# Modulation rows beside layer 0's gate and up: from column-group matmuls to VectorE, ScalarE and GpSimd

## The chip, the cores and the metric

One core of a Trainium2 chip runs the whole program in one launch. The metric is the device time of an execution in microseconds (us), lower is better; the figure of a kernel is the median of its runs. One further execution is recorded by the profiler, and all rows below come from it. The engines are TensorE (PE, with its weight loads as PEld), VectorE (DVE), ScalarE (ACT), GpSimd (POOL) and SyncE (SP), which issues the transfers spoken of here.

## What is computed

Two layers of a trunk, each with a mixer and a feed-forward part, on 1,024 latent and 128 context positions of width 1,024. What matters here is the modulation: for each layer 6 x 1,024 columns for two conditions (context and latent).

```python
silu_ctx = jax.nn.silu(c_ctx.astype(F32))
silu_c = jax.nn.silu(c.astype(F32))
for l in range(DEPTH):
    mod_ctx = (silu_ctx @ wa + ba)[None, None, :]
    mod_lat = (silu_c @ wa + ba)[:, None, :]          # wa: 1024 x 6144
    xp = layer(xp, mod_ctx, ...)
    xs = layer(xs, mod_lat, ...)

def layer(x, mod, p, ...):
    sh1, sc1, g1, sh2, sc2, g2 = jnp.split(mod, 6, axis=-1)
    h = rmsnorm(x, norm[0]) * (1.0 + sc1) + sh1
    m = mixer(h, ...)
    x = x + g1 * rmsnorm(m, norm[1])
    h = rmsnorm(x, norm[2]) * (1.0 + sc2) + sh2
    f = (silu(h @ w_gate) * (h @ w_up)) @ w_down      # hidden 2816
    return x + g2 * rmsnorm(f, norm[3])
```

The kernel multiplies the norm's weights into the modulation rows that scale (four of the six: `norm[0]` to `norm[3]` go with sc1, g1, sc2 and g2), so that such a row is (modulation + bias + 1 or 0) times a row of norm weights.

## The kernel before

The program is written with pools of buffers and a scheduler that puts each engine's instructions into a fixed order when the program is built; on the chip every engine works through its own order and waits on semaphores. The order of SP is that of the transfers. A layer goes through in-projection and mixer (phases 1 and 2), the output projection (phase 3), gate and up (`gate_up`), and the down projection (`ffn`). Layer 1's modulation rows are computed during layer 0's `gate_up`, where they aren't needed yet.

**Gate and up.** The hidden width is cut into units of 128 gate columns; `units` lists 24 of them, the first four over one half of the positions, 20 over both. A unit is a product of 2x2 blocks made with seven block products. For each, `prepare` makes the weight operand: sums of weight blocks on GpSimd (`ft`, and in place in the loaded weights; L158 is the helper for all additions of two tiles), then a split into a high part on ScalarE (L121) and a low part on VectorE (L126), both into a slot of `fw`. There are six such slots, and `prepare` runs five block products ahead of `product` (`AHEAD`). `product` runs, for each half of the positions (256 and 320 columns), 12 matmuls into one of six psum banks (`gu`; L130 to L132 are the three terms of the split), and an eviction that adds the bank to a running sum on VectorE (L158), the first of the seven a copy on ScalarE (L1449). A full unit so has 14 banks to empty, seven of 256 columns and seven of 320. After the seventh product come the tanh on ScalarE (L1456), two VectorE operations (L161) and the stores of `h` (L1461, L1463). The weights come with L1409, 512 KB each, into `fr` or spare tiles (`X`, `x`).

**Modulation beside it.** `gate_up` makes a generator `ada` and calls `next(ada)` once after each block product except a unit's first, from the fifth unit on: 120 calls. `ada_steps` goes through 24 chunks of 256 columns. A chunk's weights, 1,024 x 256, come in four loads of 256 KB into `adw` (three slots; L291). The eight row blocks are taken in two groups of four matmuls (L302): matmul j of a group uses 32 columns of the array (`tile_position`), its stationary operand is a slice of the constants that holds the silu of both conditions for its row block, and it writes 32 partitions of the bank `psada`. Then ScalarE copies the bank (L308), and `ada_total` sums: four more matmuls on the four column groups with a selection matrix as the stationary operand (L269) bring the sums of both conditions and both column halves onto one tile of 128 x 128; VectorE adds the bias row (L271), and for sc1, g1, sc2 and g2 (16 of the 24 chunks) multiplies with the norm row (L275). The bias row comes in two loads into `adr` (L264), which then holds the result; the norm row comes in two loads into a part of the `th` tile (L274); two stores bring the result to memory (`mods`, L278). `csilu` is the tile of the silu values, `konst` the constants in another layout.

In phase 1 of layer 0 the same generator computes layer 0's other rows.

Of the kernel before, what the change touches and what calls it, by code (L numbers as in the profile page):

```python
# [10 lines left out]
F32 = mybir.dt.float32  # L11
F32R = mybir.dt.float32r
I32 = mybir.dt.int32
AF = mybir.ActivationFunctionType
ALU = mybir.AluOpType
# [4 lines left out]
P = 128  # L20
L = 2
D = 1024
# [77 lines left out]
class Kern:  # L100
# [138 lines left out]
    def load_cond(self):  # L239
# [12 lines left out]
        nc.vector.tensor_reduce(out=self.sel, in_=self.ident.rearrange("p (j i) -> p i j", j=4)[:, 0:2], axis=AX.X, op=ALU.add)  # L252
        self.mods = {(l, s): self.dram([2, D], f"mod{l}_{s}") for l in range(L) for s in range(6)}

    def ada_total(self, l, c, r, ng, psp, tag, parts, by):


        nc, A = self.nc, self.A
        m = r.shape[-1]
        s, c0 = c // D, c % D  # L260
        k = {1: 0, 2: 1, 4: 2, 5: 3}.get(s)
        half = [slice(c0 + m * h, c0 + m * h + m) for h in range(2)]
        for h in range(2):
            nc.sync.dma_start(r[64 * h:64 * h + 64], A["bada"][l, s:s + 1, half[h]].broadcast_to([64, m]))  # L264
        ps = psp.tile([P, m], F32, name="psada", tag=tag)
        for h in range(2):
            for i in range(2):
                q = 64 * h + 32 * i
                nc.tensor.matmul(ps[q:q + 32], by[i], parts[i][:, m * h:m * h + m], start=True, stop=True,  # L269
                                 tile_position=(0, q))  # L270
        nc.vector.tensor_tensor(out=r, in0=ps, in1=r, op=ALU.add)  # L271
        if k is not None:
            for h in range(2):
                nc.sync.dma_start(ng[64 * h:64 * h + 64], A["normg"][l, k:k + 1, half[h]].broadcast_to([64, m]))  # L274
            nc.vector.scalar_tensor_tensor(out=r, in0=r, scalar=1.0 if s in (1, 4) else 0.0, in1=ng,  # L275
                                           op0=ALU.add, op1=ALU.mult)
        for h in range(2):
            nc.sync.dma_start(self.mods[l, s][:, half[h]], r[64 * h:64 * h + 64:32])  # L278

    def ada_steps(self, l, c0, n, pool, psp, tag, stage, bufs=2, rest=0):  # L280


        nc, A = self.nc, self.A
        quarters = [(c, q) for c in range(c0, 6 * D, n) for q in range(4)]
        ws = []

        def load():
            if len(ws) < len(quarters):
                c, q = quarters[len(ws)]
                w = pool.tile([P, 2, n], F32, name="adw", bufs=bufs)  # L290
                nc.sync.dma_start(w, A["wada"][l, 2 * q:2 * q + 2, :, c:c + n].rearrange("k p c -> p k c"))  # L291
                ws.append(w)

        for _ in range(bufs):
            load()
        for i in range(0, len(quarters), 2):
            c, q = quarters[i]
            if q == 0:
                ps = psp.tile([P, n], F32, name="psada", tag=tag)
            for j in range(4):  # L300
                kt = 2 * q + j
                nc.tensor.matmul(ps[32 * j:32 * j + 32], self.konst[:, kt:kt + 249:8], ws[i + j // 2][:, j % 2],  # L302
                                 start=q == 0, stop=q > 0, tile_position=(0, 32 * j))
            load()
            load()
            if q:
                cp = stage()[:, :n]
                nc.scalar.activation(cp, ps, AF.Copy)  # L308
            yield
            for _ in range(0 if q else rest):  # L310
                yield
            if q:
                r = pool.tile([P, n // 2], F32, name="adr")
                self.ada_total(l, c, r, cp[:, :n // 2], psp, tag, [cp] * 2,
                               [self.sel[:, k:k + 1].broadcast_to([P, 32]) for k in range(2)])
                yield
# [359 lines left out]
    def phase1(self, l):  # L676
        nc, tc, A = self.nc, self.tc, self.A
        with ExitStack() as c:
# [5 lines left out]
            adp = c.enter_context(tc.tile_pool(name="ada", bufs=1, reuse_waits="tile")) if l == 0 else None  # L684
            psp = Banks(c, tc, "ps1", {"tr": 2, "acc": 2, "psf": 3, "ad": 1} if l == 0 else {"tr": 2, "acc": 3, "psf": 3})
            if l == 0:
# [7 lines left out]
                ng = [h1p.tile([2, 512], F32, name="ng0", tag=tg) for tg in ("gc", "ginv")]  # L694
# [12 lines left out]
                for t0, n in ((0, 2), (2, 2), (4, 5)):  # L707
                    ss = h1p.tile([P, n], F32, name=f"ss0{t0}")
                    r = h1p.tile([P, n], F32, name=f"rs0{t0}")
# [7 lines left out]
                with tc.high_priority(offset=0):  # L717
                    for q in (0, 2, 1, 3):
                        ps = psp.tile([2, 512], F32, name="psada", tag="acc")
                        for j in range(4):  # L720
                            w = chunk(4 * q + j)
# [3 lines left out]
                        r = bias[q // 2][:, hs]  # L725
# [16 lines left out]
            for o in range(2):  # L742
                self.filter_spectrum(l, o, h1p, h2p, psp, "psf")
            widths = [288] + [256] * 4
            ada = self.ada_steps(0, 2 * D, 256, adp, psp, "ad",
                                  lambda: sp.tile([P, 512], F32, name="adc", tag="stg", bufs=3)) if l == 0 else iter(())

            def natural(i, kr=None):
# [630 lines left out]
    def gate_up(self, l, wr, wt, x8):  # L1379
        nc, tc, A = self.nc, self.tc, self.A  # L1380
# [3 lines left out]
        with ExitStack() as c:  # L1384
            banks = Banks(c, tc, "gu", {"ad": 2, "gu": 6})
            pool = lambda nm, bufs=1, **k: c.enter_context(tc.tile_pool(name=nm, bufs=bufs, reuse_waits="tile", **k))
# [3 lines left out]
            adp = None if last else pool("ada2")  # L1390
            x1.update({nm: pool(f"x1{nm}") for nm in ("a12", "s2", "s3", "s1", "a11")})
            if not last:
                ada = self.ada_steps(1, 0, 256, adp, banks, "ad", lambda: x8.tile([P, 2, 320], F32, name="th")[:, 0], 3, 1)
            for i, nm in enumerate(self.XOPS):
                if nm != "a12":
                    self.X[1][nm] = [x1[nm].tile([P, 4, 320], F32R, name=f"x1{nm}{h}") for h in range(2)]
            state, late = {}, []

            def load(u):

                f = units[u][0]
                if u == 1:
                    raw = [x1["a12"].tile([P, 8, P], F32, name=f"fr{i}", tag=f"x1a12{i}") for i in range(2)]
                elif u % 3 == 2 or u == 0:
                    raw = [wr.tile([P, 8, P], F32, name=f"fr{i}") for i in range(2)]
                else:
                    raw = self.spare[2 * (u % 3):][:2]
                for i in range(2):
                    nc.sync.dma_start(raw[i], A["wf"][l, f, :, 8 * i:8 * i + 8])  # L1409
                return raw  # L1410
# [54 lines left out]
            todo = [(u, i) for u in range(len(units)) for i in range(7)]  # L1465
            AHEAD = 5
            for k in range(len(todo) + AHEAD):
                if k < len(todo):
                    u, i = todo[k]
# [4 lines left out]
                if k >= AHEAD:  # L1474
                    u, i = todo[k - AHEAD]
# [252 lines left out]
```

## Time and profile before

| what | us |
|---|---|
| runs | 3404.67, 3415.93, 3424.79 |
| median | 3415.93 |
| the profiled execution | 3418.3 |
| its span in the trace | 3416.5 |
| TensorE busy in it | 3174.7 |
| VectorE, ScalarE, GpSimd busy | 2118.5, 1253.9, 439.0 |

The span is the time from the first to the last recorded instruction. A stretch of TensorE that is full at a granted clock of 1.00 can't get shorter unless it gets fewer columns to work on; the busy time of the other engines is a share of a long program with unlike stages, so the rows below are taken from the stage that changes: layer 0's gate and up runs from about 960 to 1,522 us of the profiled execution, and its modulation matmuls from 971.9 to 1,423 us.

### The profile page before, as it was taken

The numbers are of one execution on the slowest core, as the hardware profiler recorded it, in microseconds if no ns is written. First come the engines' busy times: TensorE is split into PE (matmuls) and PEld (weight loads), VectorE is DVE, ScalarE is ACT, GpSimd is POOL, SyncE is SP. The second block draws the span as 40 slices with busy tenths as digits, with TensorE's granted clock in tenths as the row PEclk, the third lists the DMA queues.
The fourth block names the chain that finished last, engine by engine and source line by source line (L and its number), as shares of the span: only waits on it lengthen the run. The fifth ranks groups of instructions, "written<-read, shape, count | busy, mean of one in ns | idle before, by whom it ended". The sixth has DMA issues, their size and how long they took to land.

```text
span 3416.5 us, 52623 instructions
## 1 busy us (share of the span) xinstructions
PE 3174.7 (93%) x19870; PEld 2795.5 (82%) x19870; DVE 2118.5 (62%) x4362; ACT 1253.9 (37%) x2340; POOL 439.0 (13%) x420
## 2 busy tenths in 40 slices
PE   8889989799979999989999999889998999998998
PEld 5768767688879999988888788778887999998887
DVE  7552752777785555564667538648777866665554
ACT  3223212566652222233433232226667322223332
POOL 0110110010042222200000011101101422220000
PEclk9999999799989999999999899999998999999999
DMA  6443554313344444345654444432052322225564
GB/s 239 142 130 119 167 160 136 114 43 115 111 135 126 136 142 127 105 157 170 199 183 135 130 129 144 145 112 73 24 163 102 107 72 72 75 66 175 184 208 137
DMA packets 357023, 444.80 MB, mean 130 GB/s; under 512 B 70707, under 2 KB 287480, under 8 KB 356001
## 3 DMA queue, kind: packets, MB, share of 16 engines
q1 hardware_dynamic: 294992, 384.46, 36.2%
q10 hardware_dynamic: 61776, 56.97, 5.4%
q8 instruction: 157, 2.57, 0.3%
q14 instruction: 98, 0.79, 0.1%
HBM read 349.32 MB, written 92.00 MB: 129 GB/s over the span
## 4 chain that ended last, share of the span: by engine, by line
PE 63%; DVE 12%; DMA 6%; ACT 5%; issue 4%; POOL 2%; SPq 0%; DVEq 0%; ACTq 0%; POOLq 0%
PE gu L130 9%; PE gu L131 9%; PE gu L132 9%; PE dq L130 4%; PE dq L132 4%; PE dq L131 4%; PE acc L130 3%; PE acc L131 3%; PE acc L132 3%; PE psada L302 2%; DMA adw<-in_wada 1%; PE pstr L944 1%; DMA dwr<-in_wf 1%; PE po L961 1%; DVE x L158 1%
## 5 line engine op out<-in xcount | busy, mean ns | idle before, releaser
L130 PE MATMUL dq<-dw 128*128 128x512 f32 x792 | 310.1, 392 | 23.2 <-ACT dw L121 22.6
L131 PE MATMUL dq<-dw 128*128 128x512 f32 x792 | 309.9, 391 | 0.0
L132 PE MATMUL dq<-dw 128*128 128x512 f32 x792 | 309.2, 391 | 0.0
L130 PE MATMUL gu<-X,fw 128*128 128x256 f32 x1024 | 289.4, 285 | 1.0 <-DVE u L158 0.7
L132 PE MATMUL gu<-X,fw 128*128 128x256 f32 x1024 | 282.8, 279 | 3.4 <-DVE fw L126 3.4
L131 PE MATMUL gu<-X,fw 128*128 128x256 f32 x1024 | 282.7, 278 | 0.0
L130 PE MATMUL acc<-whi,Th 128*128 128x256 f32 (+1 forms) x720 | 215.7, 300 | 3.9 <-ACT whi L121 3.1
L131 PE MATMUL acc<-wlo,Th 128*128 128x256 f32 (+1 forms) x720 | 213.9, 297 | 2.3 <-DVE wlo L126 2.3
L132 PE MATMUL acc<-whi,Tl 128*128 128x256 f32 (+1 forms) x720 | 212.4, 295 | 0.0
L130 PEld LDWEIGHTS gu<-X,fw 128*128 128x128 f32 x1024 | 192.3, 189 | 20.4 <-issue 10.0
L126 DVE TENSOR_TENSOR dw<-dhr,dw 128x384 fp32r<-128x384 f32 x132 | 72.4, 554 | 205.8 <-ACT dw L121 205.7
L130 PEld LDWEIGHTS dq<-dw 128*128 128x128 f32 x792 | 149.6, 189 | 56.0 <-ACT dw L121 23.1
L132 PEld LDWEIGHTS gu<-X,fw 128*128 128x128 f32 x1024 | 192.5, 189 | 3.6 <-DVE fw L126 3.6
L131 PEld LDWEIGHTS gu<-X,fw 128*128 128x128 f32 x1024 | 192.5, 189 | 0.0
L130 PE MATMUL gu<-x1s,fw 128*128 128x320 f32 x576 | 178.7, 310 | 2.9 <-DVE u L158 2.5
L126 DVE TENSOR_TENSOR dw<-dwr,dw 128x1024 fp32r<-128x1024 f32 x132 | 161.1, 1221 | 31.7 <-ACT dw L121 31.6
L132 PE MATMUL gu<-x1s,fw 128*128 128x320 f32 x576 | 178.7, 310 | 1.8 <-DVE fw L126 1.8
L131 PE MATMUL gu<-x1s,fw 128*128 128x320 f32 x576 | 178.3, 310 | 0.0
L132 PEld LDWEIGHTS dq<-dw 128*128 128x128 f32 x792 | 149.5, 189 | 31.8 <-DVE dw L126 0.7
L131 PEld LDWEIGHTS dq<-dw 128*128 128x128 f32 x792 | 149.6, 189 | 30.5
L121 ACT ACTIVATE dw<-dhr 128x384 fp32r<-128x384 f32 x132 | 67.7, 516 | 251.6 <-PE dq L132 235.8
L121 ACT ACTIVATE dw<-dwr 128x1024 fp32r<-128x1024 f32 x132 | 138.3, 1049 | 53.1 <-DMA dwr<-in_wf 44.2
(496 smaller groups left out, 8910.0 us busy)
## 6 DMA issues: line engine op xcount, KB each, us to landing
dwr<-in_wf SPq DMA_DIRECT2D x132, 512.0 KB
adw<-in_wada SPq DMA_DIRECT2D x160, 256.0 KB
dhr<-h SPq DMA_DIRECT2D x132, 192.0 KB
h<-U SPq DMA_DIRECT2D x176, 128.0 KB
X<-in_wf SPq DMA_DIRECT2D x42, 512.0 KB
fr<-in_wf SPq DMA_DIRECT2D x40, 512.0 KB
pj<-pst ACTq DMA_DIRECT2D x90, 128.0 KB
G<-gt SPq DMA_DIRECT2D x36, 256.0 KB
```

The lines of the kernel that those rows point to most:

```text
L121: nc.scalar.activation(hi, src, AF.Copy)
L126: (nc.vector if elo == "dve" else nc.gpsimd).tensor_tensor(out=lo, in0=src, in1=hi, op=ALU.subtract)
L130: mm(ps, lh, rh, start=start, stop=False)
L131: mm(ps, lh, rl, start=False, stop=False)
L132: mm(ps, ll, rh, start=False, stop=stop)
L158: (self.nc.vector if e == "v" else self.nc.gpsimd).tensor_tensor(out=out, in0=a, in1=b, op=op)
L302: nc.tensor.matmul(ps[32 * j:32 * j + 32], self.konst[:, kt:kt + 249:8], ws[i + j // 2][:, j % 2], start=q == 0, stop=q > 0, tile_position ...
L944: T(pst[:, j], pr[i][:, (k0 + j) * P:(k0 + j + 1) * P], self.ident)
L961: nc.tensor.matmul(po[:, :nq], vhl[:, k], pth[:, i, :nq], start=i == 0, stop=False)
```

## The change

The generator of before stays under the name `ada_turns` with two load slots, for phase 1 alone. `gate_up` uses a new `ada_steps`, with `dve=(0,)` and `late=3`:

- A chunk comes in eight loads of 128 KB, one for each row block, into `adw`, now two slots of 128 x 256.
- For the first condition VectorE multiplies the tile with the silu column (L167 for the first block, then L161, which also adds to the accumulator `adacc0`). For the second, ScalarE multiplies (L280 of after; the first block straight into `adacc1`, the others into `adp`), and GpSimd adds `adp` to `adacc1` (L158).
- There are four yields for a chunk: after blocks 1, 3 and 5 and at the end.
- The last sums are `ada_total` again, unchanged, with the two accumulators and a matrix of ones; they are called three yields after the chunk's end, which is behind block 5 of the next chunk.
- The bias row, later the result, is a tile of `adw`; the norm row is a tile of `adp`, which has one slot. The accumulators have two slots each.

```diff
+    def ada_steps(self, l, c0, n, pool, psp, tag, dve=(0, 1), late=0):
+        nc, A = self.nc, self.A
+        m = n // 2
+
+        def total(c, acc):
+            r, ng = (pool.tile([P, n], F32, name=nm, bufs=1 if late and nm == "adp" else 2)[:, :m]
+                     for nm in ("adw", "adw" if len(dve) > 1 else "adp"))
+            self.ada_total(l, c, r, ng, psp, tag, acc, [self.ones[:, 0:32]] * 2)
+
+        step, todo = 0, []
+        for c in range(c0, 6 * D, n):
+            acc = [pool.tile([P, n], F32, name=f"adacc{i}", bufs=2 if late else 1) for i in range(2)]
+            for kt in range(8):
+                w = pool.tile([P, n], F32, name="adw", bufs=2)
+                nc.sync.dma_start(w, A["wada"][l, kt, :, c:c + n])
+                for i in range(2):
+                    cs = self.cs[:, kt, i:i + 1]
+                    if i in dve and kt:
+                        self.stt(acc[i], w, cs, acc[i], ALU.mult, ALU.add)
+                    elif i in dve:
+                        self.ts("v", acc[i], w, cs)
+                    else:
+                        d = acc[i] if kt == 0 else pool.tile([P, n], F32, name="adp", bufs=1 if late else 2)
+                        nc.scalar.activation(d, w, AF.Copy, scale=cs)
+                        if kt:
+                            self.tt("g", acc[i], acc[i], d, ALU.add)
+                if kt == 3 or len(dve) < 2 and kt in (1, 5):
+                    step += 1
+                    if todo and todo[0][0] <= step:
+                        total(*todo.pop(0)[1:])
+                    yield
+            step += 1
+            todo.append((step + late, c, acc))
+            if not late:
+                yield
+                total(*todo.pop(0)[1:])
+            yield
+        for x in todo:
+            total(*x[1:])
...
-    def ada_steps(self, l, c0, n, pool, psp, tag, stage, bufs=2, rest=0):
+    def ada_turns(self, l, c0, n, pool, psp, tag, stage):
...
-                ada = self.ada_steps(1, 0, 256, adp, banks, "ad", lambda: x8.tile([P, 2, 320], F32, name="th")[:, 0], 3, 1)
+                ada = self.ada_steps(1, 0, 256, adp, banks, "ad", (0,), 3)
```

Outside layer 0's gate and up (with the last steps of phase 3 ahead of it) every engine's order is the same. Inside, two places show the change; the names are tiles as above, `u`, `U`, `G` and `p` the running sums of a unit, `gu` the psum banks, `h` and `mod` buffers in memory, `in_...` inputs.

On VectorE, before, where the weights of unit 16 (counted from 0; in `x_7889` and `X_7888`) are split (L126):

```order
L158 TENSOR_TENSOR G<-gu,p_12863 128x320
L126 TENSOR_TENSOR fw<-x_7889,fw 128x512
L158 TENSOR_TENSOR G<-gu,u_12865 128x256
L158 TENSOR_TENSOR G<-gu,u_12865 128x320
L271 TENSOR_TENSOR adr<-psada,adr 128x128
L126 TENSOR_TENSOR fw<-X_7888,fw 128x512
L275 SCALAR_TENSOR_TENSOR adr<-adr,th 128x128
L161 SCALAR_TENSOR_TENSOR G<-th,G 128x2x256
L161 SCALAR_TENSOR_TENSOR U<-U,G 128x2x256
L126 TENSOR_TENSOR fw<-ft,fw 128x512
```

The same place after the change (the bias addition is L313 now, in the slot of `adw`):

```order
L158 TENSOR_TENSOR G<-gu,p_13340 128x320
L313 TENSOR_TENSOR adw<-psada,adw 128x128
L161 SCALAR_TENSOR_TENSOR adacc_13076<-adw,csilu,adacc_13076 128x256
L126 TENSOR_TENSOR fw<-x_7889,fw 128x512
L158 TENSOR_TENSOR G<-gu,u_13342 128x256
L161 SCALAR_TENSOR_TENSOR G<-th,G 128x2x256
L158 TENSOR_TENSOR G<-gu,u_13342 128x320
L161 SCALAR_TENSOR_TENSOR U<-U,G 128x2x256
L161 SCALAR_TENSOR_TENSOR adacc_13076<-adw,csilu,adacc_13076 128x256
L161 SCALAR_TENSOR_TENSOR G<-th,G 128x2x320
L126 TENSOR_TENSOR fw<-X_7888,fw 128x512
L167 TENSOR_SCALAR adacc_13269<-adw,csilu 128x256
```

The steps on `adacc`, each of which reads a tile of `adw`, stand between the evictions (L158 on `gu`) and the splits. Of the 308 evictions of the stage on VectorE, the 24 last sums (L313) of after stand behind number 44, 54, 65, 73, 84, 97, 108, 119, 129, 140, 152, 164, 174, 182, 194, 204, 213, 224, 236, 248, 260, 269, 280 and 284.

On SP, before, around the loads of the weights of unit 22 (`x_7889`, `X_7888`):

```order
L291 DMA adw<-in_wada 128x2x256 x3
L274 DMA th<-in_normg 64x128 x2
L278 DMA mod_5_259<-adr 2x128 x2
L291 DMA adw<-in_wada 128x2x256 x2
L1409 DMA x_7889<-in_wf 128x1024
L264 DMA adr<-in_bada 64x128 x2
L1461 DMA h_16_210<-U 128x2x128 x2
L1409 DMA X_7888<-in_wf 128x1024
```

After, around the same two loads:

```order
L271 DMA adw<-in_wada 128x256 x5
L306 DMA adw<-in_bada 64x128 x2
L271 DMA adw<-in_wada 128x256
L316 DMA adp<-in_normg 64x128 x2
L1448 DMA x_7889<-in_wf 128x1024
L320 DMA mod_4_258<-adw 2x128 x2
L271 DMA adw<-in_wada 128x256
L1500 DMA h_16_210<-U 128x2x128 x2
L1448 DMA X_7888<-in_wf 128x1024
L271 DMA adw<-in_wada 128x256 x2
```

The row of `in_bada` takes its turn in `adw` between kt5 and kt6 of the next chunk, the norm row follows kt6, and the stores of the result (`mod`) stand ahead of kt7, which takes the slot that they free. The gate and up weights (`in_wf`) stand in the same queue.

## Rows read from the trace of the kernel before

**Rows 1.** The page: busy time, share of the span and instructions of each engine.

```profile
PE 3174.7 (93%) x19870; PEld 2795.5 (82%) x19870; DVE 2118.5 (62%) x4362; ACT 1253.9 (37%) x2340; POOL 439.0 (13%) x420
```

**Rows 2.** Three stretches: length, busy PE, PEld, DVE, ACT, POOL, clock, DMA share, GB/s.

```profile
950.00:1000.00 50.00, 36.79 (x259) 34.14 (x258) 40.30 (x71) 29.35 (x63) 22.23 (x16) 0.83 0.35 112
...
1100.00:1150.00 50.00, 50.00 (x404) 45.63 (x403) 27.87 (x56) 13.05 (x24) 10.81 (x8) 1.00 0.46 136
...
1450.00:1475.00 25.00, 25.00 (x194) 25.00 (x193) 15.37 (x29) 7.06 (x12) 6.48 (x5) 1.00 0.14 37
```

**Rows 3.** Timeline of PE from 1102 us: start, duration, instruction.

```profile
1102.38 0.31 PE L132 MATMUL gu<-x1s,fw 128*128 128x320 f32 x1
1102.62 0.43 PE L269 MATMUL psada<-th,sel 128*32 128x128 f32 x8
1102.97 0.39 PE L130 MATMUL gu<-X,fw 128*128 128x256 f32 x1
1103.20 0.28 PE L131 MATMUL gu<-X,fw 128*128 128x256 f32 x1
...
1105.97 0.31 PE L131 MATMUL gu<-x1s,fw 128*128 128x320 f32 x1
1106.12 0.31 PE L132 MATMUL gu<-x1s,fw 128*128 128x320 f32 x1
1106.36 0.67 PE L302 MATMUL psada<-adw,konst 128*32 128x256 f32 x8
1106.96 0.39 PE L130 MATMUL gu<-X,fw 128*128 128x256 f32 x1
1107.18 0.28 PE L131 MATMUL gu<-X,fw 128*128 128x256 f32 x1
1107.30 0.28 PE L132 MATMUL gu<-X,fw 128*128 128x256 f32 x1
```

**Rows 4.** Tile `psada`, 950 to 1450 us: count, ns min/median/max, first and last start.

```profile
L302 PE MATMUL psada<-adw,konst x384: 379/379/436, 971.9 to 1419.2; 128*32 128x256 f32 x192
```

**Rows 5.** Timeline, phase 1: weight loads of 256 KB issued, and their first use.

```profile
299.70 0.37 SPq L291 DMA_DIRECT2D adw<-in_wada  x1
...
302.50 0.20 PEld L302 LDWEIGHTS psada<-adw,konst 128*32 128x32 f32 x4 [0.35 <-DMA adw<-in_wada]
...
352.09 0.41 SPq L291 DMA_DIRECT2D adw<-in_wada  x1
...
355.57 0.20 PEld L302 LDWEIGHTS psada<-adw,konst 128*32 128x32 f32 x4 [2.86 <-DMA adw<-in_wada]
```

**Rows 6.** Timeline: SP's issues and VectorE's uses of small rows, and stores.

```profile
1052.65 1.06 SPq L278 DMA_DIRECT2D mod<-adr  x2
1054.78 0.52 SPq L264 DMA_DIRECT2D adr<-in_bada  x1
...
1103.11 1.11 SPq L274 DMA_DIRECT2D th<-in_normg  x2
...
1107.30 0.29 DVE L275 SCALAR_TENSOR_TENSOR adr<-adr,th 128x128 f32<-128x128 f32 x1 [1.85 <-DMA th<-in_normg]
...
1107.62 1.05 SPq L278 DMA_DIRECT2D mod<-adr  x2
```

**Rows 7.** Timeline of GpSimd, and of VectorE beside it and alone.

```profile
982.63 3.10 POOL L158 TENSOR_TENSOR x<-x 128x256 f32<-128x256 f32 x3
...
1003.05 1.62 POOL L158 TENSOR_TENSOR ft<-X,ft 128x512 f32<-128x512 f32 x1
...
1003.67 1.55 DVE L126 TENSOR_TENSOR X<-ft,X 128x512 fp32r<-128x512 f32 x1
...
1124.84 0.68 DVE L126 TENSOR_TENSOR fw<-ft,fw 128x512 fp32r<-128x512 f32 x1
```

**Rows 8.** Groups of 1050 to 1420 us with shapes apart: busy, mean ns, idle before.

```profile
L158 DVE TENSOR_TENSOR u<-gu,u 128x256 f32<-128x256 f32 x30 | 12.5, 417 | 9.0 <-PE gu L132 9.0
...
L1449 ACT ACTIVATE p<-gu 128x256 f32<-128x256 f32 x14 | 5.4, 384 | 8.7 <-PE gu L132 8.3
```

More of the change, by code (lines that the diff above doesn't have):

```diff
@@ L289, in load @@
                 c, q = quarters[len(ws)]
-                w = pool.tile([P, 2, n], F32, name="adw", bufs=bufs)
+                w = pool.tile([P, 2, n], F32, name="adw", bufs=2)
                 nc.sync.dma_start(w, A["wada"][l, 2 * q:2 * q + 2, :, c:c + n].rearrange("k p c -> p k c"))
                 ws.append(w)
-        for _ in range(bufs):
-            load()
+        load()
+        load()
         for i in range(0, len(quarters), 2):
@@ L309, in ada_steps @@
             yield
-            for _ in range(0 if q else rest):
-                yield
             if q:
@@ L744, in phase1 @@
             widths = [288] + [256] * 4
-            ada = self.ada_steps(0, 2 * D, 256, adp, psp, "ad",
+            ada = self.ada_turns(0, 2 * D, 256, adp, psp, "ad",
                                   lambda: sp.tile([P, 512], F32, name="adc", tag="stg", bufs=3)) if l == 0 else iter(())
```

## Prediction, before the change was run

> **What bounds the kernel now.** I read the page first: TensorE is busy 93% of the span, VectorE 62%, ScalarE 37%, GpSimd 13% [rows 1]. That is an average; what counts is the stage that the change touches, layer 0's gate and up. The table by stretches gives it [rows 2]: from 1100 to 1150 us TensorE is busy for the whole 50 us at a granted clock of 1.00 (2.4 GHz) while VectorE works 27.87 us, ScalarE 13.05 and GpSimd 10.81. From 1450 to 1475 us, where the modulation work is over and gate and up go on, TensorE is again full, with 194 matmuls. Only the stage's start, 950 to 1000 us, is different: TensorE 36.79 us busy, VectorE 40.30, clock 0.83.
>
> So TensorE is the bound there, and everything it issues for the modulation is paid in full. The reader should see it in the timeline of TensorE [rows 3]: the modulation's matmuls stand between two products and push the next one back. The other engines have room, 22 of 50 us on VectorE. The question is not whether the room is large enough but whether the steps that go there can follow one another fast enough: in this kernel each engine's order is fixed when it is built, so an eviction of a product's result that stands behind a modulation step on VectorE waits for that step's load.
>
> **What is removed.** Per chunk, two groups of four matmuls (L302). Two ordinary matmuls of 320 columns start 0.15 us apart; across a group the starts are 1106.12 and 1106.96, 0.84 apart, and the next spacing is 0.22 instead of 0.12 [rows 3]. That is 0.69 + 0.10 = 0.79 us for a group. The tile's row has 384 records, 8 for a group, so 48 groups [rows 4]: 48 x 0.79 = 37.9 us, all on the path since TensorE is full. The 24 ScalarE copies of the psum bank also go; ScalarE has room, so nothing.
>
> The four column-group matmuls of the last sums stay, 24 times: 0.59 and 0.23 us where 0.15 and 0.12 are ordinary [rows 3], so 0.55 us each, before and after.
>
> **What is added.** Loads of 128 KB, eight to a chunk in place of four of 256 KB, the same bytes; 192 steps of 128x256 on VectorE, 192 on ScalarE, 168 additions on GpSimd. An eviction of 128x256 takes VectorE 417 ns and a copy of that size takes ScalarE 384 [rows 8]; the steps of after have the same shape and I price them alike. By sums there is room: in the stretch without modulation work VectorE is busy 15.37 of 25 us [rows 2], and 14 evictions, a full unit, take TensorE 21.65 us (194 matmuls are 16.2 evictions of 12, so 25 / 16.2 = 1.546 us each). That is 13.3 us of VectorE's work for a unit; the order of after has 24 chunks over 240 evictions, so 11.2 steps to a unit, 4.7 us, and 0.8 us for last sums: 18.8 of 21.65.
>
> **The new chain.** What I think decides is the two slots. All weight tiles, and the bias row too, which becomes the result, share two slots of `adw`; ScalarE's products and the norm row share one slot of `adp`. Nine tiles of a chunk go through two slots in turn, and while the result holds one slot, only one is left. Followed from one chunk's last sum to the next one's:
> - The two stores of the result must land before its slot can be loaded. In the trace the bias load waits for just that: store issued 1052.65, next load 1054.78 [rows 6], 2.13 us.
> - That slot takes kt7 of the chunk. SP's queue is in order, so kt0 of the next chunk waits behind it; then kt1, kt3 and kt5 each wait until the tile before in their slot is read. A hop is a load, a read and a hand-over. The nearest loads (256 KB, TensorE the reader, queue and target the same) took 2.80 us from issue to use (299.70 to 302.50) and 3.48 (352.09 to 355.57) [rows 5]. The read is 0.42, the hand-over 0.03 (VectorE ends 1107.59, the store is issued 1107.62 [rows 6]). So 3.25 to 3.93; I take the mean, 3.59, since nothing says which of the two is usual.
> - For a chunk with a norm row, the row's slot is `adp`, free only when GpSimd has added the product of kt5: a fourth hop, and an addition of 0.81 to 1.03 us (half of 1.62 for 128x512, a third of 3.10 for three of 128x256 [rows 7]); I take 0.9. Then the norm row itself: issued 1103.11, used 1107.30, 4.19 us, and 0.29 for the last step [rows 6]. Sum: 2.13 + 4 x 3.59 + 0.9 + 4.19 + 0.32 = 21.9 us.
> - For a chunk without: the bias row is issued behind kt5's load (0.4 us of issue), and I give it the norm row's 4.19. Sum: 2.13 + 3 x 3.59 + 0.4 + 4.19 + 0.32 = 17.8 us.
>
> Against that stands the time that the order of after leaves: from the first last sum to the 23rd there are 236 evictions of `gu` on VectorE, 22 periods, 15 with a norm row (about 11.1 evictions each) and 7 without (9.9). At TensorE's pace they take 236 x 1.546 + 22 x 0.55 = 377.0 us. The chain needs 15 x 21.9 + 7 x 17.8 = 453.1. Since last sum and evictions are in one order on VectorE, the stage gets longer by the difference, 76.1 us. With 2.80 us loads the periods are 20.5 and 16.8, together 425, so 48 more than TensorE needs; with 3.48 us loads 23.3 and 18.8, 481, so 104 more. Here the work that covers the loads is six psum banks of evictions and the weight splits made five products ahead, 5 x 3.09 = 15 us; that takes up one late load, not a rate that is too slow. Behind a waiting step stand the evictions (VectorE), the splits that feed the next product (ScalarE, VectorE) and, on SP, the gate and up weights themselves; their lateness is the same wait seen elsewhere and I don't count it again.
>
> By the Trainium skill, DMA: Bandwidth & Descriptors, "Anatomy of one DMA", a transfer costs some 2.0 us fixed and its bytes at 436 GB/s, on the queue that GpSimd drives: 2.3 us for 128 KB. By that price, an estimate, a hop is 2.75 us, the periods 18.5 and 15.3, the stage 8 to 12 us over TensorE's, and the change a gain of some 24. The rows at hand, on SP's queue, are 0.5 to 1.2 us longer.
>
> **The start.** The first modulation steps of after stand on VectorE among the steps that end phase 3 and the first splits, where VectorE, not TensorE, sets the pace [rows 2]. A load that is not there costs up to two hops, 8 us, there; their 11 or so steps cost 0.42 each, and where GpSimd works beside, nothing may be lost: 1 to 8 us, I take 4.
>
> **Sum.** The profiled execution took 3418.3 us; -37.9 + 76.1 + 4 gives 3460.5, and it is 2.4 over the median 3415.9, so **3458 us**. Low end of this case: 48 and 1, 3427. High end: 104 and 8, and 1 us a chunk (22 us) for steps that find VectorE or ScalarE busy with a split, 3512.
>
> **Rivals.**
> *TensorE stays the bound* (the other side). If loads are quick enough that the chain needs no more than 17.8 us for a period with a norm row and 15.8 without, the evictions never wait: -37.9 + 4 gives 3382. For it: the order of after was laid out with these very spacings, and 128 KB is half of what the rows show. Against: even with the quickest load and the smallest addition the chain with a norm row is 20.4 us, 2.6 too long, so each of its four loads would have to be there in 2.15 us. Between the two cases the sign turns at a hop of 3.07 us (15 x 4 + 7 x 3 = 81 hops, 42 us less): below that the change gains. Chance 0.20.
>
> *VectorE becomes the bound through GpSimd.* Where GpSimd ran without a break, a 128x512 split took VectorE 1.55 us; beside an idle GpSimd 0.68 [rows 7]. In after GpSimd adds 9.8 times a unit; if each held VectorE up for 0.9 us, a unit is 18.8 + 8.8 = 27.6 us against TensorE's 22.4: 17 units x 5.2 = 88 us, 3468 at most; if a third do, nothing beyond 3382. The Trainium skill, SBUF — State Buffer, "Who interferes with whom", says that a VectorE operation with two SBUF inputs shares a read port with GpSimd and that the one that comes second is blocked; by that rule the new steps, which read weights and accumulator from SBUF, are all open to it, and the trace's 1.55 against 0.68 agrees. Alone it gives 3380 to 3430: the additions wait for ScalarE, so they are spread out and half of VectorE's work reads psum. Chance 0.12, most of it near no change.
>
> *The chain decides, as forecast*: 0.68, of which 0.07 within 0.5%.
>
> **Chances and range.** 0.5% is 17 us, about what a measurement of this kernel can tell from no change. Slower: 0.61 of the forecast and 0.03 of the VectorE case, 0.64. Faster: 0.17 and 0.03, 0.20. Within: 0.07, 0.03, 0.06, 0.16. The range for 8 in 10 leaves out the lower half of TensorE's case and what is beyond the chain's high end: 3385 to 3525. The likeliest case alone: 3427 to 3512.
>
> **What would show it.** Right: TensorE's share between 1000 and 1500 us falls to about 85%; the longest waits of VectorE's modulation steps end with a load of `adw`, `adp` or with SP's store; 128 KB loads take 2.8 to 3.5 us from issue to use; last sums come 20 to 23 us apart. Wrong: loads under 2.5 us, last sums 17 us apart, TensorE full; or VectorE near 90% busy, with 128x256 steps of 0.8 us and more and no waits for loads; or other stages changed, which the order gives no reason for.

## The result

The changed kernel takes 3465.24 us (median of four runs, 3463.35 to 3465.62) against 3415.63 before: ratio 1.0144, 95% interval 1.0118 to 1.0170. It is slower by 49.6 us. Forecast were 3458 and the range 3385 to 3525.

The page of the profiled execution (3465.6 us, span 3463.8) against [rows 1]: TensorE does less, every other engine more, GpSimd most of all.

```profile
PE 3159.5 (91%) x19486; PEld 2806.6 (81%) x19486; DVE 2234.9 (65%) x4554; ACT 1329.3 (38%) x2508; POOL 587.9 (17%) x588
```

The stage itself, by stretches (columns as in [rows 2]). First the kernel before, 1000 to 1500 us:

```profile
1000.00:1500.00 500.00, 498.53 (x3946) 462.17 (x3944) 295.49 (x550) 142.09 (x254) 114.19 (x84) 1.00 0.41 120
```

The changed kernel, two pieces and the same 500 us:

```profile
1100.00:1150.00 50.00, 43.43 (x325) 41.42 (x326) 41.55 (x74) 20.31 (x40) 27.52 (x27) 1.00 0.39 118
...
1200.00:1250.00 50.00, 43.82 (x312) 42.32 (x311) 35.89 (x64) 19.32 (x38) 22.75 (x23) 0.93 0.39 117
1000.00:1500.00 500.00, 448.02 (x3230) 429.12 (x3229) 375.35 (x678) 196.76 (x382) 243.57 (x232) 0.95 0.38 115
```

TensorE is idle for 52 of 500 us where it was idle for 1.5, and its granted clock is 0.95 where it was 1.00. GpSimd's busy time has doubled. The first down-projection matmul (`dq`), which follows the stage, starts at 1576.1 us instead of 1522.4, 53.7 us later. The profiled executions as wholes are 47.3 us apart, since what follows is 6.4 us shorter; so all of the loss is in this stage.

What TensorE and the others waited for, 990 to 1560 us (engine and line, what ended the wait, us in total, times, longest):

```profile
ACT adp L280 <- DMA adw<-in_wada: 90.9, 50, 5.2
...
ACT adp L280 <- POOL adacc L158: 58.2, 59, 3.5
...
PE psada L311 <- DVE adacc L161: 46.1, 20, 4.6
DVE adacc L161 <- DMA adw<-in_wada: 32.3, 43, 2.7
...
DVE adw L317 <- DMA adp<-in_normg: 7.6, 9, 2.4
...
PE gu L130 <- DVE u L158: 6.1, 4, 3.9
```

The third row is the one that costs: TensorE stands at the first matmul of the last sums (L311) until VectorE has finished the chunk's last accumulation. Banks of `gu`, where I expected the wait, cost it 6.1 us and a few rows of 2 to 3.

One period of the chain, from the timeline of all engines, modulation rows alone (start, duration, engine and line, in brackets the idle time before and what ended it):

```profile
1214.38 0.29 DVE L317 SCALAR_TENSOR_TENSOR adw<-adw,adp 128x128 f32<-128x128 f32 x1 [0.20 <-DMA adp<-in_normg]
1214.70 1.05 SPq L320 DMA_DIRECT2D mod<-adw  x2
...
1215.91 3.06 SPq L271 DMA_DIRECT2D adw<-in_wada  x3
1218.08 0.51 ACT L280 ACTIVATE adp<-adw,csilu 128x256 f32<-128x256 f32 x1 [2.20 <-POOL ft L158]
1218.10 0.48 DVE L161 SCALAR_TENSOR_TENSOR adacc<-adw,csilu,adacc 128x256 f32<-128x256 f32 x1 [0.70 <-DMA adw<-in_wada]
...
1218.73 0.38 PE L311 MATMUL psada<-adacc,konst 128*32 128x128 f32 x2 [2.15 <-DVE adacc L161]
...
1222.27 0.83 POOL L158 TENSOR_TENSOR adacc<-adacc,adp 128x256 f32<-128x256 f32 x1 [2.88 <-ACT adp L280]
1222.43 0.96 DVE L161 SCALAR_TENSOR_TENSOR adacc<-adw,csilu,adacc 128x256 f32<-128x256 f32 x1
1225.47 0.47 DVE L161 SCALAR_TENSOR_TENSOR adacc<-adw,csilu,adacc 128x256 f32<-128x256 f32 x1
...
1236.39 0.29 DVE L317 SCALAR_TENSOR_TENSOR adw<-adw,adp 128x128 f32<-128x128 f32 x1
```

From one norm step to the next it is 22.0 us. A load of 128 KB is used 2.2 us after its issue (1215.91 to 1218.08). The matmul of the last sums at 1218.73 starts right behind the step of 1218.10, after 2.15 us of idle time. The step at 1222.43 takes 0.96 us beside GpSimd's addition of 1222.27; the next one, with GpSimd idle, 0.47.

### The profile page after: what moved, and what is told of

Same layout as the page of the kernel before. It is cut to its first block, busy times and chain, and to the rows that moved or that the text cites. A ratio compares the mean times of both kernels' runs of the same rounds, so it can differ in the third digit from the quotient of the medians.

```text
span 3463.8 us, 52815 instructions
## 1 busy us (share of the span) xinstructions
PE 3159.5 (91%) x19486; PEld 2806.6 (81%) x19486; DVE 2234.9 (65%) x4554; ACT 1329.3 (38%) x2508; POOL 587.9 (17%) x588
## 4 chain that ended last, share of the span: by engine, by line
PE 54%; DVE 13%; DMA 9%; ACT 5%; issue 5%; POOL 4%; SPq 1%; DVEq 0%; ACTq 0%; POOLq 0%
PE gu L132 5%; PE gu L131 5%; PE gu L130 5%; PE dq L132 4%; PE dq L130 4%; PE dq L131 4%; DMA adw<-in_wada 4%; PE acc L130 2%; PE acc L131 2%; PE acc L132 2%; POOL adacc L158 1%; PE pstr L983 1%; PE wo L130 1%; PE wo L132 1%; DVE adacc L161 1%
## 5 line engine op out<-in xcount | busy, mean ns | idle before, releaser
L126 DVE TENSOR_TENSOR dw<-dhr,dw 128x384 fp32r<-128x384 f32 x132 | 72.4, 554 | 209.0 <-ACT dw L121 208.8
L130 PEld LDWEIGHTS gu<-X,fw 128*128 128x128 f32 x1024 | 196.8, 193 | 8.0 <-issue 5.6
L132 PEld LDWEIGHTS gu<-X,fw 128*128 128x128 f32 x1024 | 196.6, 193 | 4.9 <-DVE fw L126 4.4
L131 PEld LDWEIGHTS gu<-X,fw 128*128 128x128 f32 x1024 | 197.0, 193 | 0.6 <-issue 0.6
L130 PE MATMUL gu<-x1s,fw 128*128 128x320 f32 x576 | 183.5, 319 | 8.5 <-DVE u L158 6.4
L158 POOL TENSOR_TENSOR adacc<-adacc,adp 128x256 f32<-128x256 f32 x168 | 150.9, 898 | 212.2 <-ACT adp L280 211.9
L132 PE MATMUL gu<-x1s,fw 128*128 128x320 f32 x576 | 183.0, 318 | 1.6 <-DVE fw L126 1.5
L131 PE MATMUL gu<-x1s,fw 128*128 128x320 f32 x576 | 182.8, 317 | 0.0
L126 DVE TENSOR_TENSOR dw<-dwr,dw 128x1024 fp32r<-128x1024 f32 x132 | 161.0, 1221 | 31.0 <-ACT dw L121 30.8
```

Of the source, the lines that this page charges most:

```text
L126: (nc.vector if elo == "dve" else nc.gpsimd).tensor_tensor(out=lo, in0=src, in1=hi, op=ALU.subtract)
L130: mm(ps, lh, rh, start=start, stop=False)
L131: mm(ps, lh, rl, start=False, stop=False)
L132: mm(ps, ll, rh, start=False, stop=stop)
L158: (self.nc.vector if e == "v" else self.nc.gpsimd).tensor_tensor(out=out, in0=a, in1=b, op=op)
```

## The experiments

All times are medians; a ratio is that to the kernel before, run beside it (3414.9 to 3420.5 us).

**What the removed matmuls were worth, and the floor.**

```diff
 # before_without_groups (from the kernel before)
...
-            for j in range(4):                       # matmuls L302
+            for j in range(0 if rest else 4):
...
-                nc.scalar.activation(cp, ps, AF.Copy)
+                nc.scalar.activation(cp, ws[i + 1][:, 1] if rest else ps, AF.Copy)
```

> The kernel before with the 48 groups of matmuls left out in gate and up (ScalarE copies a loaded weight tile where it copied the psum bank; layer 1's modulation rows are not the reference's); loads, copies, last sums and rows stay. It measures the first term of the forecast alone: 37.9 us less, 3378 (3370 to 3390). Rival (something else takes the place of the matmuls as the bound): 3395 to 3416.

Measured 3372.52 us, 0.9883 (0.9859 to 0.9907): 44 us less.

```diff
 # no_modulation (from the changed kernel)
-                ada = self.ada_steps(1, 0, 256, adp, banks, "ad", (0,), 3)
+                ada = iter(())      # and six plain stores into mods
```

> After with no modulation work at all beside gate and up (layer 1's modulation rows are norm weights in place of modulation, so the output is another). It is the floor of the stage: the forecast's prices give 48 x 0.79 = 38 and 24 x 0.55 = 13 us under before, 3365 (3355 to 3380). If the stage has another bound beside TensorE's columns, 3385 or more.

Measured 3357.74 us, 0.9844 (0.9813 to 0.9876), some 15 us under the one above. Both prices on TensorE stand. What the change adds therefore costs 3465.2 - 3372.5 = 93 us (89 by the ratios).

**The shared slots.**

```diff
 # rows_apart
-            r, ng = (pool.tile([P, n], F32, name=nm, bufs=1 if late and nm == "adp" else 2)[:, :m]
-                     for nm in ("adw", "adw" if len(dve) > 1 else "adp"))
+            r, ng = tail()[:, 640:768], tail()[:, 768:896]   # unused end of the tanh tile
...
```

> After's modulation work, but the bias row with the result and the norm row have a place of their own (the unused tail of the tile that holds the tanh), so the two slots of adw hold weights alone and adp products alone. Theory (the chain through the shared slots is too slow): a chunk then needs four hops of 3.59 us, 14.4 us, against 9.33 banks of 1.546 us and 0.55 for the last sums, 15.0; TensorE is nearly full, the waits at the last sums' matmuls are gone, 3375 to 3400 us. Rival (128 KB loads one behind the other, or VectorE and GpSimd in each other's way, are too slow whoever holds the slots): 3440 to 3465.

Measured 3431.85 us, 1.0043 (1.0024 to 1.0063): 33 us of the 93 are gone, not the 65 to 90 that I expected. The waits at the last sums are gone as forecast, but TensorE now waits for evictions. Its waits in this kernel, 990 to 1530 us:

```profile
PE gu L130 <- DVE G L158: 24.7, 31, 1.6
PE gu L130 <- DVE u L158: 7.7, 10, 3.9
```

```diff
 # third_slot (rows_apart, and)
-                w = pool.tile([P, n], F32, name="adw", bufs=2)
+                w = slots()[(c // n * 8 + kt) % 3]     # the third in the tanh tile; norm row in adp again
...
```

> As the kernel before it, but the weights have three slots and the norm row is back in the one slot of adp. Theory: hops overlap by three, the chain is 10 us a chunk or less and the norm row's 4.2 us stand beside it: 3370 to 3390, no worse than two slots. If the norm row in adp is what stops the chain: 3400 to 3440, and ScalarE waits for the norm row's step.

3426.12 us, 1.0035 (1.0020 to 1.0050). The 6 us under rows_apart lie inside both intervals; the 35 to 55 that were still to go stay. The time is in the range of the second case, the norm row in `adp`. But ScalarE waits little for the norm row's step (L323) and far more for GpSimd's additions, so that case isn't shown. Its waits, 990 to 1530 us:

```profile
ACT adp L286 <- POOL adacc L158: 118.7, 109, 3.5
...
ACT adp L286 <- DVE thx L323: 11.7, 10, 4.7
```

**Where TensorE stands.**

```diff
 # sums_of_constants
-            self.ada_total(l, c, r, ng, psp, tag, acc, [self.ones[:, 0:32]] * 2)
+            self.ada_total(l, c, r, ng, psp, tag, [self.konst] * 2, [self.ones[:, 0:32]] * 2)
```

> After, but the matmuls of the last sums read constants in place of the two accumulators (layer 1's modulation rows are then not the reference's); everything else, the slots and the loads too, is as in after. Theory as forecast (evictions on VectorE stand behind steps that wait for the chain): TensorE loses the wait at the last sums' matmuls and waits as long for banks of gu, 3445 to 3470. Rival (TensorE's own queue is where it is lost, since its matmuls stand right behind the chunk's last accumulation): 3380 to 3400, and VectorE's evictions never make it wait.

3444.27 us (3430 to 3448 in four runs, the profiled one 3430), 1.0073 (1.0044 to 1.0102): just under the first case, some 21 us less than the changed kernel. TensorE's longest waits in this kernel (990 to 1530 us):

```profile
PE psada L311 <- DVE adw L313: 29.0, 11, 5.3
PE gu L130 <- DVE u L158: 7.9, 8, 3.9
```

With no operand to wait for it waits for a psum bank, which VectorE's bias step has to empty, and that step waits for the chain. So the place of the wait in TensorE's queue is worth a part; the chain behind it keeps the rest.

**The engines without the loads.**

```diff
 # no_loads (rows_apart, and)
-                w = pool.tile([P, n], F32, name="adw", bufs=2)
-                nc.sync.dma_start(w, A["wada"][l, kt, :, c:c + n])
+                w = held[kt % 2]                       # two tiles, loaded once
...
```

> As the first kernel of this row, but the weight tiles are loaded once and used for all steps (layer 1's modulation rows are then not the reference's): the 192 VectorE, 192 ScalarE and 168 GpSimd steps and the small rows stay, the 190 loads go. Theory: the engines' steps themselves fit, 3370 to 3390. Rival (VectorE bound by GpSimd's additions): 3400 to 3460, VectorE near 90% busy in the stage with no waits for loads.

3417.74 us, 0.9995 (0.9975 to 1.0015): only 14 us under rows_apart, although no weight is waited for any more. The rival holds: VectorE.

```diff
 # no_loads_no_adds (no_loads, and)
-                        if kt:
-                            self.tt("g", acc[i], acc[i], d, ALU.add)
```

> As no_loads, and GpSimd's 168 additions left out as well; VectorE's and ScalarE's steps stay (the modulation rows are not the reference's). If VectorE and GpSimd in each other's way is what keeps no_loads at 3418: VectorE's steps fall from 0.85 us to 0.49, its busy share from 93% to 80% or less, and the time to 3370 to 3390. If VectorE's own 192 steps are too much, whoever runs beside them: 3405 to 3420.

3385.90 us, 0.9922 (0.9898 to 0.9946): the 168 additions on GpSimd cost 32 us there, VectorE's and ScalarE's own steps 13. ScalarE waits 190 us for the additions in no_loads, so part of the 32 may go by that and not by VectorE; no run parts the two there. Stretches of 1100 to 1400 us in the changed kernel, in no_loads and in no_loads_no_adds, in this order:

```profile
1100.00:1400.00 300.00, 263.53 (x1896) 252.38 (x1897) 223.96 (x411) 119.58 (x233) 147.57 (x145) 0.94 0.39 116
```
```profile
1100.00:1400.00 300.00, 277.19 (x2106) 262.65 (x2105) 279.07 (x460) 134.90 (x270) 162.81 (x167) 1.00 0.26 73
```
```profile
1100.00:1400.00 300.00, 298.60 (x2341) 290.38 (x2341) 265.16 (x523) 103.72 (x194) 71.89 (x54) 1.00 0.28 80
```

In no_loads VectorE is busy 279 of 300 us and does 460 operations; without the additions it does 523 in 265 us, and TensorE is full. That is 88% and not the 80% that I expected. The steps themselves, from the groups of the same 300 us (busy, mean ns of one), again in this order:

```profile
L161 DVE SCALAR_TENSOR_TENSOR adacc<-adw,csilu,adacc 128x256 f32<-128x256 f32 x101 | 70.6, 699 | 19.0 <-DMA adw<-in_wada 18.4
```
```profile
L161 DVE SCALAR_TENSOR_TENSOR adacc<-adh,csilu,adacc 128x256 f32<-128x256 f32 x121 | 102.9, 850 | 2.1
```
```profile
L161 DVE SCALAR_TENSOR_TENSOR adacc<-adh,csilu,adacc 128x256 f32<-128x256 f32 x138 | 87.7, 636 | 2.4
```

I had priced a step at 0.42 us. Without the additions it fell to 0.64 on the mean and not to the 0.49 that I expected, because GpSimd's weight sums are still there. The single steps of these 300 us show it: the 106 during which GpSimd has no operation take 0.47 to 0.49 us, the 32 beside a weight sum 1.15 on the mean. In the changed kernel the 38 with GpSimd idle also take 0.47 to 0.49, and the 55 beside an addition 0.85 on the mean, up to 1.62.

**Which operand.**

```diff
 # sum_in_psum (rows_apart with three slots, and)
-                        self.stt(acc[i], w, cs, acc[i], ALU.mult, ALU.add)
+                        self.stt(pacc, w, cs, pacc, ALU.mult, ALU.add)   # psum; the last block writes SBUF
...
```

> A whole version: rows apart, three slots of weights, and VectorE's accumulator in a psum bank until the chunk's last block, so that a step reads one operand from SBUF and one from psum. If the two engines' shared access is what makes the steps slow: they take 0.42 to 0.5 us as the evictions do, and the time falls below third_slot's 3426 to 3385 to 3405, faster than both kernels. If it is the number of steps or the rate of GpSimd's chain: 3415 to 3430.

3413.77 us, 1.0000 (0.9983 to 1.0017). The steps do what was expected; the time falls by 12 us from third_slot, to just under the second case. Part of the 12 may be the norm row, which third_slot has in `adp` and this kernel in the tanh tile. The groups of VectorE and of GpSimd in this kernel, 1100 to 1400 us:

```profile
L161 DVE SCALAR_TENSOR_TENSOR pacc<-adw,csilu,pacc 128x256 f32<-128x256 f32 x103 | 50.0, 486 | 15.5 <-DMA adw<-in_wada 13.6
L126 DVE TENSOR_TENSOR fw<-ft,fw 128x512 fp32r<-128x512 f32 x30 | 22.2, 738 | 14.9 <-ACT fw L121 14.1 <-POOL adacc L158 0.6
L126 DVE TENSOR_TENSOR fw<-X,fw 128x512 fp32r<-128x512 f32 x20 | 16.5, 823 | 10.2 <-ACT fw L121 10.1
```
```profile
L158 POOL TENSOR_TENSOR adacc<-adacc,adp 128x256 f32<-128x256 f32 x121 | 97.8, 809 | 94.7 <-ACT adp L283 87.9 <-ACT adacc L283 6.8
```

GpSimd adds as often as in no_loads and nearly as long (843 ns there), and the steps take 486 ns: with the accumulator in psum they don't feel it. The 84 steps beside an operation of GpSimd take 0.47 to 0.49 us, as the others do. The splits, with both operands in SBUF, still do (0.74 and 0.82 us, [rows 7]: 0.68 alone), and now wait 24 us for ScalarE, which stands in its own queue behind products whose loads or slot are late.

**The additions in the changed kernel itself.** The edit of no_loads_no_adds alone, made in the changed kernel:

> After with GpSimd's 168 additions left out (layer 1's modulation rows are not the reference's); slots, loads, VectorE's and ScalarE's steps as in after. If the price of the additions (32 us between no_loads and no_loads_no_adds) stands beside that of the shared slots: 3433. If the slots' chain sets the pace and covers it, so that only the addition ahead of the norm row counts (0.9 us in 15 periods): 3445 to 3460. If the additions are what makes the chain itself long: under 3425.

3420.10 us, 1.0005 (0.9989 to 1.0021): 45 us less, more than the 32 of no_loads: the third of the cases. In the changed kernel the additions lengthen the chain itself: 22 periods, from result to result, take 412 us here and 466 there. TensorE still waits at the last sums (990 to 1530 us), and a step is 0.10 us shorter on the mean (1100 to 1400 us):

```profile
PE psada L309 <- DVE adacc L161: 31.5, 19, 3.9
```
```profile
L161 DVE SCALAR_TENSOR_TENSOR adacc<-adw,csilu,adacc 128x256 f32<-128x256 f32 x110 | 66.0, 600 | 24.4 <-DMA adw<-in_wada 23.4 <-DVE u L158 0.3
```

```diff
 # after_two_adp (the changed kernel, and)
-                        d = acc[i] if kt == 0 else pool.tile([P, n], F32, name="adp", bufs=1 if late else 2)
+                        d = acc[i] if kt == 0 else product()   # adp and the tail of the tanh tile in turn
...
```

> After with a second place for ScalarE's products and the norm row (the tail of the tanh tile), so that ScalarE can make the next product while GpSimd adds; all 168 additions stay, and the bias row and result still share adw with the weights. If the additions cost what they do because ScalarE waits for the one slot of adp (58 us of its idle time in after): the time falls most of the way to that without additions (3420), 3420 to 3440. If they cost it because VectorE's and GpSimd's operations hold each other up: 3450 to 3465, and VectorE's steps stay near 0.7 us.

3466.24 us, 1.0153 (1.0128 to 1.0177), nothing gained. ScalarE's wait for GpSimd falls from 58.2 us to 7.7, as intended, but TensorE's waits (990 to 1560 us) and VectorE's steps (1100 to 1400 us) are those of the changed kernel:

```profile
PE psada L318 <- DVE adacc L161: 44.5, 19, 5.5
...
ACT adp L287 <- POOL adacc L158: 7.7, 3, 3.0
```
```profile
L161 DVE SCALAR_TENSOR_TENSOR adacc<-adw,csilu,adacc 128x256 f32<-128x256 f32 x104 | 72.3, 695 | 20.5 <-DMA adw<-in_wada 20.1
```

So the additions don't cost by the one slot alone in which ScalarE hands its products over.

**A version that beats both.** Rows apart, three slots of weights, both accumulators in one psum bank on VectorE; ScalarE and GpSimd keep only the second condition's first blocks.

```diff
 # mixed_3 (mixed_4: kt < 4)
-            acc = [pool.tile([P, n], F32, name=f"adacc{i}", bufs=2 if late else 1) for i in range(2)]
+            acc, pacc, part = [None, None], psp.tile([P, 2, n], F32, name="pacc", tag=tag), None
...
+                    if i and kt < 3:                   # ScalarE; GpSimd adds the second and third
+                        d = pool.tile([P, n], F32, name="adp" if kt else "adpart")
+                        nc.scalar.activation(d, w, AF.Copy, scale=cs)
...
+                        self.stt(o, w, cs, part if i and kt == 3 else pacc[:, i], ALU.mult, ALU.add)
```

> A whole version: rows apart, three slots of weights, both accumulators in a psum bank on VectorE; ScalarE and GpSimd take only the second condition's first three blocks, so 48 additions in place of 168, and 312 steps of VectorE in place of 192. By the measured prices: 13 us for steps over the 3372 without the groups, and most of the 32 us of additions gone: 3385 to 3400, faster than both kernels. If VectorE's 312 steps are the bound (312 x 0.49 = 153 us beside some 310 of its own work in 520): 3405 to 3425. If loads behind one another are what is left: 3400 to 3415, and VectorE and ScalarE wait for adw.

> As mixed_3 with four blocks of the second condition on ScalarE and GpSimd: 72 additions, 288 steps. If GpSimd's additions cost 32 / 168 = 0.19 us each and a step of VectorE less: 1 to 6 us over mixed_3; if VectorE's number of steps is the bound, up to 12 us under it.

mixed_3: 3384.18 us, 0.9892 (0.9873 to 0.9912), 81 us under the changed kernel and some 36 under the one before, with every modulation row computed. mixed_4: 3390.16 us, 0.9915 (0.9898 to 0.9932): 24 additions more, 24 steps less, 6 us more (3378 to 3387 us in the runs of mixed_3, 3388 to 3397 in those of mixed_4). mixed_3 from 1100 to 1400 us:

```profile
1100.00:1400.00 300.00, 292.67 (x2275) 282.73 (x2274) 271.29 (x594) 98.23 (x193) 98.99 (x89) 1.00 0.48 141
```

VectorE does 594 operations in 271 us where no_loads did 460 in 279. TensorE is nearly full. It is 12 us over before_without_groups (3 by the ratios).

## Why the prediction was right, and where not

**Sign, size and period: right.** The last sums' bias steps (L313) stand between 1054.3 and 1528.6 us, 23 periods of 20.6 us on average; of the first 22 the 15 with a norm row are 21.7 us long (forecast 21.9), the 7 without 20.0 (forecast 17.8). Together 465 us, forecast 453, against 377 that TensorE would need. The stage got 53.7 us longer; the forecast's terms gave 42. TensorE's busy share from 1000 to 1500 us is 90%, not 85. One of my signs of being wrong was there, loads under 2.5 us, and the sums came as far apart as forecast all the same.

**The removed matmuls: right.** 37.9 us forecast, 44 measured; the last sums 13 and 15.

**The shared slots: right as a cause, too large.** Giving the rows a place of their own took 33 us away (rows_apart), not the whole of 76. A hop there, from the issue of a load to the end of the tile's last read, is 4.09 us on the mean, so that a chunk's four hops are 16.4 us against the 15.0 that TensorE needs; I had expected 14.4. The steps that were wrong:

*A load.* I took 3.14 us for it, the mean of two rows at 256 KB. At 128 KB it is 2.2 us from issue to use: the median of the 103 reads that waited for a load of weights between 1050 and 1530 us. By my own formula, 81 hops 0.97 us shorter are 79 us, and the forecast would have been that the sign turns. The Trainium skill, DMA: Bandwidth & Descriptors, "Anatomy of one DMA", gives 2.3 us for that size, an estimate, by its fit for GpSimd's queue; the measured 2.2 on SP's queue is near it, and my rows were of twice the size. I had put this price beside the sum and not believed it.

*The reading.* I took 0.42 us, one read by VectorE as soon as the tile is there. But a tile of `adw` has two readers, and its slot is free when the second is done. One such hop in the changed kernel, from the timeline of all engines:

```profile
1226.12 1.92 SPq L271 DMA_DIRECT2D adw<-in_wada  x2
...
1228.55 0.74 POOL L158 TENSOR_TENSOR adacc<-adacc,adp 128x256 f32<-128x256 f32 x1
1228.65 0.92 DVE L161 SCALAR_TENSOR_TENSOR adacc<-adw,csilu,adacc 128x256 f32<-128x256 f32 x1
...
1229.32 0.51 ACT L280 ACTIVATE adp<-adw,csilu 128x256 f32<-128x256 f32 x1 [0.45 <-POOL adacc L158]
...
1229.86 1.16 SPq L306 DMA_DIRECT2D adw<-in_bada  x2
```

The tile issued at 1226.12 is read by VectorE at 1228.65 and by ScalarE at 1229.32, once GpSimd has freed the slot for the product; the bias row then takes the tile's slot, 3.74 us after the issue. Over the 175 loads issued between 1050 and 1530 us the first read starts 2.97 us after the issue on the mean and the second ends at 4.08; in 104 of them ScalarE is the last. So a hop as a whole was longer than the 3.59 of the forecast: the load 0.9 us less, the reading 1.4 more. The two errors cancel, and with them the period came right.

*The stores.* I had said that kt7 takes the slot that the result's stores free. In the trace its load is issued 1.2 us after the first store (1214.70 to 1215.91), and it is kt0's load that waits for the stores to land, 2.09 us (the second of the three loads in the row of 1215.91 above, issued at 1216.79). In periods with a norm row, counted from result to result, 1.7 us go to the load of kt7 (forecast 2.2), 12.0 to the hops of kt7, kt1 and kt3 (10.8), and 8.1 from kt5's load to the next result (9.0).

*GpSimd.* I had its hold on VectorE as a rival of its own (0.12), asking whether VectorE's sum of work becomes the bound. (That rival's 3468 should be 3470, 3382 + 88.) It isn't in the changed kernel (375 of 500 us busy), but the chain runs through VectorE's steps and ScalarE's products, so what GpSimd does to them counts there long before an engine is full. Without the additions a hop is 3.53 us instead of 4.08, by my formula 81 x 0.55 = 45 us, and the kernel is 45 us faster. With a second slot for the products a hop is still 3.96 us: ScalarE no longer waits, but VectorE is then the last reader (119 of 176). The Trainium skill, SBUF — State Buffer, "Who interferes with whom", says that VectorE needs the read interface it shares with GpSimd for a second SBUF operand; the runs agree (0.85 us with two operands in SBUF, 0.49 with one in psum, GpSimd adding in both).

How the 0.55 us of a hop divide between the longer steps (0.10 of them on the mean), the longer splits in VectorE's queue and ScalarE's waits, no run here separates; the edit also lets the scheduler place things anew.

**The place of the wait: wrong.** I had the evictions on VectorE behind late steps, and TensorE out of banks. It waits in its own queue, at L311, 46.1 us for VectorE and 5.1 for GpSimd. "Three steps later" does not hold there: in TensorE's order the matmuls of the first seven chunks stand 4 to 18 banks behind the accumulation that they read, from the eighth to the 23rd 0.6 to 2.8. I take it that the chain falls behind the calls that make it already when the order is built, so that they are put down as soon as their operand should be there, with no room; no run shows this. In rows_apart the same distance is 11 to 12 banks from the third chunk to the 23rd, and that wait is gone. A few banks of room don't help when the chain is late: with 4 to 5 of them TensorE still waits 1.5 to 4.6 us at the fifth to the seventh chunk. sums_of_constants shows how much hangs on the place alone: some 21 us of 93.

**The clock: not in the forecast.** TensorE's granted clock was 1.00 in this stage [rows 2] and is 0.94 from 1100 to 1400 us now. The timeline of TensorE in the changed kernel shows it:

```profile
1177.01 0.38 PE L311 MATMUL psada<-adacc,konst 128*32 128x128 f32 x2 [2.42 <-DVE adacc L161]
...
1179.03 0.42 PE L131 MATMUL gu<-X,fw 128*128 128x256 f32 x1
1179.24 0.41 PE L132 MATMUL gu<-X,fw 128*128 128x256 f32 x1
...
1182.31 0.30 PE L131 MATMUL gu<-x1a,fw 128*128 128x320 f32 x1
1182.45 0.31 PE L132 MATMUL gu<-x1a,fw 128*128 128x320 f32 x1
```

And the granted clock of two stretches of it:

```profile
1179.00:1182.00 3.00, 3.00 (x16) 3.00 (x15) 2.95 (x6) 2.04 (x5) 0.00 (x0) 0.50 0.27 84
1183.00:1187.00 4.00, 4.00 (x32) 4.00 (x31) 2.21 (x4) 1.73 (x4) 2.25 (x3) 1.00 0.82 250
```

Behind a pause of 2.42 us matmuls of 256 columns start 0.21 us apart instead of 0.12, at 0.50 (1.2 GHz), for some 3 us. Of the 300 us from 1100 to 1400, 34 were granted 0.50, and TensorE was busy in 32 of them: at full speed some 16 us less. Not every pause has such a stretch behind it: after one of 2.58 us, which ended at 1135.2, the clock stayed at 1.00. In rows_apart, whose pauses are short (1.6 us at most for the commonest), it is 1.00. No run takes the clock apart from the pauses.

**The start: not separable.** I gave it 4 us; the stretch 950 to 1000 us has TensorE busy 33.8 us instead of 36.8, some 3 us.

So the chain through the slots was there as forecast, and the number came out within 8 us by luck: a load priced too high made up for a reading priced too low, and for a clock that I did not have. The ladder of the runs is the better account: 13 us for steps, 32 for additions beside them, 14 for loads, 33 for the shared slots, together 3372.5 to 3465.2. Its single prices are good to some 7 us (by the ratios the additions are 25) and depend on the order of the rungs: the additions are 32 us in no_loads and 45 in the changed kernel.

## What to carry to other kernels

Work moved from a full engine to idle ones is priced by the chain it forms, not by their free time: write down one period, with each slot that two kinds of data share, and set it against what the full engine needs in that time. Time a hop by a transfer of its own size, count every reader that must be done before the slot is free and what that reader waits for, and time a step by what runs beside it: with two SBUF operands on VectorE a step beside GpSimd's additions took nearly twice as long. Moving an accumulator to psum and leaving GpSimd out of most of the sum turned a loss of 50 us into a gain of 36.

## What the runs showed of the hardware beyond this

The same step of 128x256 on VectorE (L161, SCALAR_TENSOR_TENSOR) with both operands in SBUF took 0.47 to 0.49 us with GpSimd idle and 0.85 on the mean beside its additions; with the accumulator in psum it took 0.47 to 0.49 beside them too. A late operand at one matmul mostly cost twice: the pause itself, and a stretch at 1.2 GHz behind it.
